# Issuing the weight-piece loads from ScalarE's queue in a hybrid decoder step

## The chip, the cores and the metric

The kernel runs on one core of one Trainium2 chip. The metric is the device time of one execution in microseconds (us), lower is better. All times below come from the profile of the kernel before, or from its timed runs.

## What is computed

One inference step of one decoder layer, in float32, for a prompt of 2048 tokens (width 1024) and for a sample group of 8 single tokens with states carried in. The layer projects each token with `w_in` (1024 x 3336), splits the result into eight RWKV-7 heads and eight Mamba-2 heads, runs both recurrences, concatenates, projects with `w_out` (1024 x 1024), adds the scaled input and normalises, then runs a squared-ReLU MLP with `w_ff1` (1024 x 4096) and `w_ff2` (4096 x 1024), adds and normalises again. Outputs are both token groups and all new states. In outline:

```python
proj = x @ w_in
o_r, wkv = rwkv7_mix(shifted(proj[:1792]), ...)
o_m, conv, ssm = mamba2_mix(proj[1792:], ...)
h = layer_norm(ALPHA * x + concat(o_r, o_m) @ w_out)
y = layer_norm(ALPHA * h + square(relu(h @ w_ff1)) @ w_ff2)
```

## The kernel before

The prompt is cut into four blocks of 512 tokens. The first stage projects the four blocks one after the other (`project`, L358 on), with the mixers of block 0 set between its matmuls. Then each block has a tail (`tail`): the `w_out` product, the first normalisation, 32 transposes into the layout that the MLP wants, the MLP in groups of four hidden tiles, the second normalisation. While the tail of one block runs, the mixers of the next block (RWKV chunks, Mamba chunks, the post-processing) are set between its matmuls by `drive`, and the sample group's work rides along in the first tail. The last tail has no mixers beside it.

Every large matmul is done in a split form for accuracy: an operand is held as a high and a low half (float32r), and three matmuls (`mm3`, L166, L167, L168) make one product. So every weight has to be split on the chip. This is done piece by piece, each time it is used, by `wpiece`: a piece of 128 partitions x 512 (256 KB) is loaded into a tile of the pool `wr` (L206); ScalarE copies it with rounding to the high half of a tile of the pool `w` (L199, in `split`); VectorE, or GpSimd for every fourth piece of the projection and every second one of the first part of a tail (`POOLA`, `POOLO`), subtracts that from the raw piece for the low half (L200). TensorE then reads both halves. The pool `wr` has 7 buffers and the pool `w` has 8, so a load can start when the subtraction seven pieces earlier in that pool is done, and a copy can start when TensorE has read the piece eight earlier.

The activations take the same way: `load_act` loads slices of x or of the mixers' output into the same pool `wr` (L322), and `split` makes the halves. The weights of a step that does not go through `wpiece` (`wdt`, L353; the small up-projections, L290) are loaded elsewhere.

All transfers are issued by SyncE (SP): weight pieces, x and mixer slices, and the mixers' scratch transfers, which move tiles through DRAM to change their layout: eight stores (L640) and eight loads (L645) per RWKV chunk, chunk loads (L621 to L626), broadcasts (L539, L542), Mamba loads (L802, L804), stores of outputs (L1229, L1165), and so on. SP works through its queue in order: an issue that waits for a buffer holds everything behind it. So do the other engines.

The order of each engine's queue is not written by hand. The tile framework orders the instructions when the program is built, from their priority (place in the program) and its own estimate of when each can start; it also sets the semaphore waits. ScalarE's queue holds the copies, the evictions of the projections (L425, L475, L476), the relu and square of the MLP (L1454, L1455), the normalisations (L1221), the transposes' evictions (L1346) and the small copies of the recurrence (L720, L732, L700).

Of the kernel before, what the change touches and what calls it, by code (L numbers as in the profile page):

```python
# [108 lines left out]
class K:  # L109
# [92 lines left out]
    def wpiece(self, src, shape, tag="w"):  # L202

        n = int(np.prod(shape))
        raw = self.sb(tag + "r", (128, 512))
        self.nc.sync.dma_start(raw[:, :n], src)  # L206
        hl = self.sb(tag, (128, 2, 512), F32R)
        self.npiece += 1
        r = {"a": POOLA, "o": POOLO, "f": POOLF}[self.pf]
        pool = r and self.npiece % r == 0  # L210
        self.split(raw[:, :n], hl[:, 0, :n], hl[:, 1, :n], self.nc.gpsimd if pool else None)
        return [hl[:, i, :n].rearrange("p (a b) -> p a b", a=shape[0]) for i in range(2)]
# [1416 lines left out]
```

## Time and profile before

| | |
|---|---|
| time, median of 3 runs | 2891.64 us (2886.47 to 2894.46) |
| the profiled execution's own time | 2881.87 us |
| its span, first to last instruction | 2880.1 us |
| mean granted TensorE clock | 0.982 of full speed |
| TensorE matmuls busy | 2786.3 us, 97% |
| VectorE busy | 1979.4 us, 69% |
| ScalarE busy | 1285.9 us, 45% |
| GpSimd busy | 364.5 us, 13% |
| 16 DMA engines, hardware queue | 45.4% |

The profiled execution is 9.8 us (0.3%) below the median of the timed runs. A busy share counts the time in which at least one instruction of that kind runs on the engine; waiting, and the issuing of a transfer, does not count. PEclk in the rows is the granted clock of TensorE: 1.00 is 2.4 GHz and 0.50 is 1.2 GHz, and a number between them is a mean over the stretch.

### The profile page before, as it was taken

To read this page: it belongs to the slowest core of one execution; us is meant where nothing else is said; L and a number is where in the kernel's file an instruction comes from. 1 tells how busy PE (TensorE), PEld (TensorE's weight loads), DVE (VectorE), ACT (ScalarE), POOL (GpSimd) and SP (SyncE) were. 2 spreads that over 40 slices of the span, in tenths; PEclk is the share of its full clock that TensorE was granted. 3 is DMA by queue.
4 is the path that set the end of the run, shared out by engine and by line. 5 is a ranking of instruction groups with operands and counts; after the bars stand their busy time and mean duration, and the time that the engine had idled before them with its cause. 6 is when DMAs were issued, how large, how long until landed. Compare 5 with 4: busy or idle time off the path is not lost.

```text
span 2880.1 us, 52319 instructions
## 1 busy us (share of the span) xinstructions
PE 2786.3 (97%) x19114; PEld 2310.9 (80%) x19114; DVE 1979.4 (69%) x4841; ACT 1285.9 (45%) x2493; POOL 364.5 (13%) x508
## 2 busy tenths in 40 slices
PE   9999999999989999998899999998999999899997
PEld 7798987777878777787788888887777778888886
DVE  7878878878777767676866666568766656754446
ACT  5554644554536333434544444336343334543332
POOL 2322212222321000002200000022000001200001
PEclk9999999999989999998999999999999999899999
DMA  6655655555744434346434344254443335433232
GB/s 207 191 169 150 185 152 165 156 176 160 211 138 133 131 110 130 110 125 215 136 93 120 115 116 121 85 196 131 120 138 114 109 103 167 158 103 95 88 103 70
DMA packets 333766, 395.54 MB, mean 137 GB/s; under 512 B 84990, under 2 KB 191060, under 8 KB 333500
## 3 DMA queue, kind: packets, MB, share of 16 engines
q1 hardware_dynamic: 333508, 392.20, 45.4%
q8 instruction: 150, 2.46, 0.4%
q14 instruction: 108, 0.88, 0.1%
HBM read 331.32 MB, written 60.81 MB: 136 GB/s over the span
## 4 chain that ended last, share of the span: by engine, by line
PE 79%; DVE 10%; DMA 4%; issue 4%; ACT 2%; SPq 1%; POOL 0%; DVEq 0%; POOLq 0%; ACTq 0%
PE psb L166 18%; PE psb L167 18%; PE psb L168 17%; PE psm L152 7%; PE psa L166 4%; PE psa L168 4%; PE psa L167 4%; PE psc L152 2%; PE psa L152 2%; PE psb L152 1%; DVE w L200 1%; PE psm L173 1%; PE psy L741 1%; DVE lr L655 1%; DVE rX L656 1%
## 5 line engine op out<-in xcount | busy, mean ns | idle before, releaser
L199 ACT ACTIVATE w<-wr 128x512 fp32r<-128x512 f32 (+1 forms) x836 | 518.8, 627 | 604.5 <-PE psb L168 237.2
L200 DVE TENSOR_TENSOR w<-wr,w 128x512 fp32r<-128x512 f32 x712 | 510.8, 722 | 230.3 <-ACT w L199 226.5
L166 PE MATMUL psb<-act,w 128*128 128x512 f32 (+2 forms) x1768 | 628.4, 356 | 6.3 <-ACT act L199 5.5
L167 PE MATMUL psb<-act,w 128*128 128x512 f32 (+2 forms) x1768 | 621.1, 352 | 0.6 <-DVE act L200 0.6
L168 PE MATMUL psb<-act,w 128*128 128x512 f32 (+2 forms) x1768 | 616.9, 349 | 0.0
L166 PEld LDWEIGHTS psb<-act,w 128*128 128x128 f32 x1768 | 335.9, 190 | 55.5 <-ACT act L199 6.0
L168 PEld LDWEIGHTS psb<-act,w 128*128 128x128 f32 x1768 | 336.3, 190 | 45.6 <-DVE w L200 0.2
L167 PEld LDWEIGHTS psb<-act,w 128*128 128x128 f32 x1768 | 337.0, 191 | 44.7 <-DVE act L200 2.6
L166 PE MATMUL psb<-w,g 128*128 128x512 f32 x788 | 317.0, 404 | 9.5 <-ACT w L199 9.5
L167 PE MATMUL psb<-w,g 128*128 128x512 f32 x788 | 314.6, 399 | 0.0
L168 PE MATMUL psb<-w,g 128*128 128x512 f32 x788 | 312.5, 397 | 0.0
L200 POOL TENSOR_TENSOR w<-wr,w 128x512 fp32r<-128x512 f32 x124 | 180.2, 1458 | 717.5 <-ACT w L199 703.6
L1504 DVE TENSOR_TENSOR g<-psb,g 128x512 f32<-128x512 f32 x173 | 118.8, 687 | 163.2 <-PE psb L168 162.6
L166 PEld LDWEIGHTS psb<-w,g 128*128 128x128 f32 x788 | 148.6, 189 | 46.1 <-ACT w L199 10.3
L168 PEld LDWEIGHTS psb<-w,g 128*128 128x128 f32 x788 | 148.4, 188 | 33.6 <-DVE g L200 0.2
L167 PEld LDWEIGHTS psb<-w,g 128*128 128x128 f32 x788 | 149.0, 189 | 32.5 <-DVE w L200 0.2
L200 DVE TENSOR_TENSOR g<-r,g 128x256 fp32r<-128x256 f32 (+1 forms) x172 | 97.1, 565 | 82.5 <-ACT g L199 81.6
L1454 ACT ACTIVATE r<-psb 128x512 f32<-128x512 f32 (+2 forms) x130 | 63.2, 487 | 190.2 <-PE psb L168 188.3
L166 PE MATMUL psa<-act,w 128*128 128x256 f32 (+2 forms) x336 | 116.4, 346 | 0.0
L167 PE MATMUL psa<-act,w 128*128 128x256 f32 (+2 forms) x336 | 114.6, 341 | 0.0
L168 PE MATMUL psa<-act,w 128*128 128x256 f32 (+2 forms) x336 | 114.1, 340 | 0.0
L655 DVE TENSOR_TENSOR lr<-rX,lr 128x4 f32<-128x4 f32 (+14 forms) x480 | 100.7, 210 | 10.8
(389 smaller groups left out, 5207.3 us busy)
## 6 DMA issues: line engine op xcount, KB each, us to landing
wr<-in_w_ff_dram SPq DMA_DIRECT2D x512, 256.0 KB
wr<-in_w_in_dram SPq DMA_DIRECT2D x208, 256.0 KB
wr<-in_w_out_dram SPq DMA_DIRECT2D x112, 256.0 KB
lr<-d_l SPq DMA_DIRECT2D x256, 64.0 KB
s_m<-g SPq DMA_DIRECT2D x48, 256.0 KB
ms<-s_m SPq DMA_DIRECT2D x16, 768.0 KB
wr<-in_xT_dram SPq DMA_DIRECT2D x32, 256.0 KB
s_ar<-g SPq DMA_DIRECT2D x16, 512.0 KB
```

The source lines that it names most:

```text
L152: return self.nc.tensor.matmul(out, l, r, start=start, stop=stop)
L166: nc.tensor.matmul(out, l[0], r[0], start=first, stop=False)
L167: nc.tensor.matmul(out, l[0], r[1], start=False, stop=False)
L168: nc.tensor.matmul(out, l[1], r[0], start=False, stop=last)
L173: self.nc.tensor.transpose(out, in_, self.cst[p0:p0 + k, o + p0:o + p0 + k])
L199: nc.scalar.activation(hi, raw, AF.Copy)
L200: (eng or nc.vector).tensor_tensor(out=lo, in0=raw, in1=hi.bitcast(F32), op=ALU.subtract)
L655: nc.vector.tensor_tensor(out=row, in0=X[:, :, s + 1:16], in1=row, op=ALU.mult)
L656: nc.vector.tensor_reduce(X[:, :, s:s + 1], lr[:, :, 17 * s:16 * s + 16], axis=AX.X, op=ALU.add)
L741: acc = lambda o, l, r, start, stop: nc.tensor.matmul(o, l, r, start=start, stop=stop, skip_group_check=True)
L1454: nc.scalar.activation(rl, ps, AF.Relu)
L1504: self.nc.vector.tensor_tensor(out=h, in0=ps, in1=h, op=ALU.add)
```

## The change

The load in `wpiece` (L206) is issued from ScalarE's queue in place of SP's. That is 832 loads of 256 KB: 208 of `w_in`, 112 of `w_out` and 512 of the two MLP matrices. All other transfers stay on SP, those into the pool `wr` by `load_act` and `wdt` among them. No buffer count and no arithmetic changes.

```diff
 raw = self.sb(tag + "r", (128, 512))
-self.nc.sync.dma_start(raw[:, :n], src)
+self.nc.scalar.dma_start(raw[:, :n], src)
 hl = self.sb(tag, (128, 2, 512), F32R)
```

## Rows read from the trace of the kernel before

**Rows 1.** The first line of the page: busy time, share of the span and number of instructions of each engine.

```profile
PE 2786.3 (97%) x19114; PEld 2310.9 (80%) x19114; DVE 1979.4 (69%) x4841; ACT 1285.9 (45%) x2493; POOL 364.5 (13%) x508
```

**Rows 2.** Busy time by stage: the stretch in us from the span's start, its length, then the busy time and number of instructions of each engine, the granted TensorE clock, the share of the DMA engines, and GB/s.

```profile
0.00:775.00 775.00, 757.38 (x5110) 624.41 (x5111) 612.61 (x1505) 393.60 (x737) 187.71 (x338) 1.00 0.60 174
775.00:885.00 110.00, 96.06 (x881) 88.23 (x879) 74.61 (x209) 46.40 (x92) 26.32 (x25) 0.89 0.46 144
885.00:1300.00 415.00, 412.20 (x2757) 327.95 (x2753) 292.79 (x747) 171.50 (x330) 13.70 (x22) 1.00 0.43 125
1300.00:1460.00 160.00, 141.08 (x1018) 122.99 (x1017) 119.96 (x279) 82.88 (x167) 34.12 (x27) 0.88 0.49 161
1460.00:1940.00 480.00, 475.64 (x3850) 405.87 (x3850) 306.57 (x813) 205.11 (x460) 32.17 (x37) 1.00 0.41 121
1940.00:2030.00 90.00, 80.12 (x633) 70.02 (x632) 77.56 (x197) 54.10 (x111) 16.46 (x13) 0.94 0.45 146
2030.00:2430.00 400.00, 397.92 (x2790) 315.81 (x2789) 256.38 (x677) 154.83 (x291) 17.05 (x24) 1.00 0.39 118
2430.00:2530.00 100.00, 90.54 (x645) 84.52 (x644) 73.06 (x140) 55.40 (x105) 25.98 (x16) 0.91 0.47 160
2530.00:2800.00 270.00, 270.00 (x1171) 218.77 (x1169) 118.68 (x178) 101.71 (x172) 0.00 (x0) 1.00 0.33 101
```

**Rows 3.** The waits of TensorE's matmuls over the whole span: who waited <- for whom, us in total, times, longest us.

```profile
PE psb L166 <- ACT w L199: 13.9, 5, 9.3
PE psb L173 <- DVE g L1308: 9.9, 4, 4.7
PE psb L166 <- ACT act L199: 5.5, 2, 5.2
PE psb L167 <- DVE w L200: 4.4, 1, 4.4
```

**Rows 4.** The view of line L206, the loads that the change moves: count, duration of one issue on SP's queue in ns (shortest/median/longest), start of the first and the last in us; and the first line of who waited for their landing (us, times).

```profile
L206 SPq DMA_DIRECT2D wr<-in_w_ff_dram x512: 327/328/1325, 839.7 to 2826.9; - x171
L206 SPq DMA_DIRECT2D wr<-in_w_in_dram x208: 327/382/1230, 0.7 to 750.5; - x104
L206 SPq DMA_DIRECT2D wr<-in_w_out_dram x112: 327/332/1325, 756.0 to 2469.8; - x112
...
  ACT w L199: 47.3, 42
```

**Rows 5.** The view of the tiles `wr`: the copies on ScalarE and the two kinds of subtraction, with duration in ns (shortest/median/longest).

```profile
L199 ACT ACTIVATE w<-wr x836: 239/632/655, 3.5 to 2843.3; 128x512 fp32r<-128x512 f32 x168
L200 DVE TENSOR_TENSOR w<-wr,w x712: 209/691/1793, 4.2 to 2844.0; 128x512 fp32r<-128x512 f32 x178
...
L200 POOL TENSOR_TENSOR w<-wr,w x124: 1262/1302/2252, 13.6 to 2489.5; 128x512 fp32r<-128x512 f32 x124
```

**Rows 6.** The waits of SP's queue ahead of these loads: us in total, times, longest us.

```profile
SPq L206 <- DVE w L200: 594.9, 319, 31.9
...
SPq L206 <- POOL w L200: 55.9, 50, 4.2
```

**Rows 7.** The three largest kinds of wait of ScalarE: us in total, times, longest us.

```profile
ACT w L199 <- PE psb L168: 237.2, 167, 8.5
ACT r L1454 <- PE psb L168: 188.3, 104, 13.3
ACT w L199 <- PE psa L168: 175.2, 52, 8.5
```

**Rows 8.** The busy time of the instructions on tiles `wr` alone, summed over the four stretches 775 to 885, 1300 to 1460, 1940 to 2030 and 2430 to 2530 us.

```profile
sum 460.00, DVE 80.68 ACT 97.32 POOL 85.89; mean DVE 20.17 ACT 24.33 POOL 21.47
```

**Rows 9.** SP's queue from 825 us in order of time: start, us, engine, line, operation, out<-in, count.

```profile
825.65 3.62 SPq L640 DMA_DIRECT2D d_l<-sc  x8
829.37 4.50 SPq L645 DMA_DIRECT2D lr<-d_l  x8
833.96 2.74 SPq L206 DMA_DIRECT2D wr<-in_w_out_dram  x6
```

**Rows 10.** From the chain of work in the same stretch: start, us, transfer.

```profile
833.45 2.26 DMA lr<-d_l
835.85 3.57 DMA wr<-in_w_out_dram
```

**Rows 11.** Busy time from 845 to 875 us, columns as in Rows 2.

```profile
845.00:875.00 30.00, 27.55 (x195) 25.30 (x195) 20.10 (x66) 15.51 (x35) 5.07 (x5) 0.77 0.58 187
```

**Rows 12.** SP's queue around 1308 us in order of time, ahead of the weight loads that follow the first tail's last wait.

```profile
1307.10 1.09 SPq L1068 DMA_DIRECT2D d_y<-lr  x2
1308.29 0.54 SPq L322 DMA_DIRECT2D wr<-s_o  x1
1308.88 0.90 SPq L206 DMA_DIRECT2D wr<-in_w_ff_dram  x2
```

**Rows 13.** The start of the span in order of time: SP's first and second weight load, and TensorE's first matmul with the wait ahead of it in brackets.

```profile
0.73 0.40 SPq L206 DMA_DIRECT2D wr<-in_w_in_dram  x1
...
3.07 0.43 SPq L206 DMA_DIRECT2D wr<-in_w_in_dram  x1
...
5.19 0.79 PE L166 MATMUL psb<-act,w 128*128 128x512 f32 x1 [5.19 <-ACT act L199]
```

**Rows 14.** SP's queue in the first stage: an instruction that the program has only in the sample group's work (L1200), which the code reaches after all four projections.

```profile
36.12 0.80 SPq L1200 DMA_DIRECT2D out_dram<-in_state_conv_dram  x1
```

## The prediction, made before the changed kernel was run

> **What bounds the kernel now.** I read the engines' shares first [rows 1]. TensorE's matmuls are busy 97% of the span; VectorE stands at 69%, ScalarE at 45%. So the bound is TensorE, and a change on another engine moves the time only where it makes TensorE wait or ends a wait. The table by stage [rows 2] says where that is. Idle is length minus matmul time. In the four long stretches between the changes of stage (885 to 1300, 1460 to 1940, 2030 to 2430, 2530 to 2800) it is 2.8, 4.4, 2.1 and 0.0 us, 9.3 us in 1565 us. In the four short stretches at the start of each tail's transposes and MLP (775 to 885, 1300 to 1460, 1940 to 2030, 2430 to 2530) it is 13.9, 18.9, 9.9 and 9.5 us: 52.2 us in 460 us, with the clock at 0.88 to 0.94. The first 775 us lose 17.6 us. The rest lies after the last weight load. The reader is to see that only the short stretches, and a little of the first stage, can answer to this change.
>
> Next, who ends TensorE's waits [rows 3]. The largest kind is a weight copy of ScalarE, 13.9 us, but 9.3 us of it is one wait; then a VectorE addition, 9.9 us; the start-up, 5.5 us nearly all in one; and one late subtraction, 4.4 us. No steady wait on ScalarE shows. Last, the loads themselves [rows 4]: copies waited for their landing 47.3 us in 42 cases out of 832 loads, and those are waits of ScalarE, not of TensorE. The loads run far enough ahead.
>
> **The change part by part.**
>
> *Removed from SP:* 832 issues. Their medians are 328 ns for 512, 382 ns for 208 and 332 ns for 112 [rows 4]: 168 + 79 + 37 = 284 us. With the longer ones among them I take 0.38 us each, 317 us. SP computes nothing, so this is worth something only where another SP transfer, or a weight load behind one, was late for TensorE. I find three places. At 825 us, sixteen scratch issues take 3.62 + 4.50 us and six weight loads stand behind them [rows 9]; the matmul that then waits 4.4 us waits for a weight's subtraction [rows 3]. At 1307 us, two sample stores and one slice load stand ahead of the weight loads until 1308.88 [rows 12], and the 9.3 us wait falls there; the slot is freed by a subtraction of VectorE, so only about 1.2 us of it is SP's. At the start, the second weight load goes out at 3.07 us behind slice loads [rows 13]; TensorE starts at 5.19 us and waits there for an activation slice, so I give 0.5 us. Sum of the three: 6.1 us at most. I take 4 us, since in the first place VectorE is busy with the recurrence too.
>
> Here the trace and a rule part. SP's sixteen issues took 8.1 us, while the load behind them landed in 2.26 us and a weight load in 3.57 us [rows 9, 10]: issuing was the longer part. The Trainium skill, page "DMA: Bandwidth & Descriptors", section "Issuing engines are not separate DMA queues", says that transfers of all issuing engines share the same DMA engines and that issuing from several saves only sequencer time, usually small beside the transfer. By the page the credit would be near nothing and the sum 9 us over the median where the rows make it 5; the rows measure this kernel, so I go by them.
>
> *Added to ScalarE:* 832 issues in its queue. No row shows an issue on ScalarE. Lower bound: nothing, if ScalarE's sequencer issues while the engine finishes an activation. Upper bound: the 317 us of SP's rows. I take SP's price, the nearest row. ScalarE then goes from 1286 to 1603 us, 56% of the span. What covers it: in the long stretches ScalarE is itself waiting for TensorE. It waited 237.2 + 175.2 us for a free `w` tile and 188.3 us for a matmul result ahead of a relu [rows 7]; an issue of 0.38 us in front of a relu that waits 1.8 us on average (188.3 / 104) costs nothing. Those stretches lost 9.3 us in 1565 us and I add nothing there. In the short stretches, work on pieces and slices takes ScalarE 97.32 us [rows 8]; at 632 ns each [rows 5] that is 154 copies, so about 154 issues, 59 us. ScalarE goes there from 238.8 us (the sum of four rows) to 298 of 460 us, 65%, still under VectorE's 345 us, 75% [rows 2]. If each issue delayed TensorE, 59 us; if none, 0. TensorE is idle 11% of these stretches (52.2 / 460), and I charge the issues at that share: 7 us. In the first stage, 208 issues at 0.38 are 79 us; TensorE is idle 2.3% there (17.6 / 775): 2 us.
>
> *A wait moved:* each of these issues waits until the subtraction seven loads earlier has freed the slot. On SP this was a wait of 594.9 us in 319 cases for VectorE and 55.9 us in 50 cases for GpSimd [rows 6], and held nothing that computes. On ScalarE it holds evictions, copies and the recurrence's small copies, for which TensorE waits. It is free if the issue stands in ScalarE's queue at a point where the subtraction is done anyway. That the order is made so shows in SP's queue, which takes what is ready and not what the program has next: a transfer of the sample group goes out at 36.12 us, in the first stage [rows 14]. A subtraction lasts 0.69 us on VectorE and 1.30 us on GpSimd [rows 5]. I charge nothing for this part and price the other case below.
>
> *Bytes* stay as they are, and so does the depth of the buffers.
>
> **Sum.** 2881.9 us of the profiled execution (span 2880.1) + 7 + 2 - 4 = 2887 us. The median of the timed runs is 9.8 us above the profiled execution; on its scale the forecast is 2891.6 + 5 = **2897 us**, 0.2% more. A measurement of this kernel can tell about 0.3%, 8.7 us, from no change, so this is no measurable change.
>
> **The rivals.**
>
> *Slower: the slot wait blocks ScalarE.* Place: the four short stretches, where half the subtractions of a tail's first part go to GpSimd, and VectorE is 75% busy. If 38% of the issues (319 / 832) meet a wait of 1.86 us (594.9 / 319), 154 of them add 59 waits, 110 us, beside 59 us of issuing: ScalarE comes to 408 of 460 us, 89%, and passes VectorE. If TensorE sees a quarter of the 169 us, 42 us: 2934 us. For it: the wait on SP is real, and ScalarE's evictions of the transposes stand in the same queue. Against it: SP reaches each wait early because it has nothing else to do, so its 1.86 us are too long for ScalarE. It decides where ScalarE's share in these stretches passes VectorE's.
>
> *Faster: SP was holding TensorE.* The 4.4 us wait at 840 us goes, with 1.2 us at 1308 and 0.5 us at the start. Behind the first, the clock is 0.77 for 30 us [rows 11]; if the wait goes and the clock stays at 2.4 GHz, 0.23 x 30 = 7 us more. 2891.6 - 13 = 2879 us. For it: sixteen issues in a row ahead of weight loads occur once per chunk. Against it: VectorE's waits remain in the same places, and a clock falls for them as well.
>
> *The run-ahead is lost.* If the order put each issue right ahead of its own copy, every copy would wait for a landing of 3.57 us [rows 10]: 832 x 3.57 = 2970 us on top of 1286, and the kernel would take over 4200 us. SP's order [rows 14] speaks against it. 2 in 100, left out of the range.
>
> **How the numbers follow.** No measurable change 0.38, slower 0.34 (of it 0.02 for the lost run-ahead), faster 0.28. A new order of all queues, by the framework's own estimate, can move single waits of 5 us either way; that is why the middle case does not get more. The range runs from two waits like that at 840 us saved (2 x 12 = 24 us under the median, 2868) to the slower rival with a little more of its 169 us seen (54 us over, 2945). Of the middle case the own range is 2883 to 2900.
>
> **What would show it.** After the change, SP's queue has no L206 and ScalarE's has 832 of them, at 0.3 to 0.4 us. ScalarE's busy time stays near 1286 us, since issuing does not count. Right: the long stretches lose under 15 us again and TensorE's waits for ScalarE stay near 20 us; the 4.4 us wait for a subtraction is gone or smaller. Wrong to the slow side: new waits of ScalarE at L206 for VectorE or GpSimd, and TensorE's waits for evictions (L1346, L1454) or small copies (L720, L732) over 20 us in total, or idle time in the long stretches. Wrong to the fast side: the short stretches lose under 40 us and their clock is above 0.95. An issue of 1 us or more on ScalarE would break the price on which all of this rests.

## The result: 0.7% slower

The changed kernel takes 2906.59 us, median of 8 runs (2898.02 to 2913.48), beside 2885.81 us for the kernel before on the same chip (8 runs). The ratio is 1.0068, 95% interval 1.0052 to 1.0085: some 20 us, more than twice the 8.7 us that the prediction took as the least to be told from no change. The profiled execution took 2901.37 us, with a span of 2899.5 us and a mean granted clock of 0.983 (0.982 before).

The first line of the page after, beside [rows 1]: the busy time of TensorE rises by 6.4 us. Its idle time, span minus busy, rises from 93.8 to 106.8 us. That makes up the 19.4 us by which the span grew. No other engine got busier; ScalarE shows nothing of its 832 issues, since issuing is not counted.

```profile
PE 2792.7 (96%) x19114; PEld 2311.2 (80%) x19114; DVE 1977.0 (68%) x4841; ACT 1277.9 (44%) x2493; POOL 358.6 (12%) x508
```

The loads after, beside [rows 4], with the same columns. The issues stand in ScalarE's queue (ACTq) with a median of 0.33 us. The first line is the one to read: 516 semaphore instructions ahead of loads, up to 2.53 us long, now in ScalarE's queue. When the queue comes to one of them it stands until the slot is free. SP's queue had 736 of them before, up to 31.8 us long, and held nothing that computes.

```profile
L206 ACTq EVENT_SEMAPHORE  x516: 17/17/2530, 15.3 to 2556.9; - x172
L206 ACTq DMA_DIRECT2D wr<-in_w_ff_dram x512: 333/334/1612, 836.2 to 2847.2; - x171
L206 ACTq DMA_DIRECT2D wr<-in_w_in_dram x208: 334/335/1491, 0.7 to 768.4; - x104
L206 ACTq DMA_DIRECT2D wr<-in_w_out_dram x112: 334/335/1672, 771.7 to 2496.1; - x112
...
  ACT w L199: 69.0, 52
```

The table by stage after, with the columns of [rows 2]. The last lines cover the same clock times, not quite the same work, since the kernel lags by up to 20 us.

```profile
0.00:775.00 775.00, 750.99 (x5059) 619.30 (x5060) 604.37 (x1495) 386.91 (x726) 177.06 (x334) 0.99 0.59 170
775.00:885.00 110.00, 98.51 (x862) 89.53 (x861) 77.03 (x213) 50.13 (x97) 31.26 (x28) 0.95 0.56 169
885.00:1300.00 415.00, 409.63 (x2790) 326.15 (x2789) 289.81 (x747) 170.69 (x334) 14.66 (x22) 1.00 0.44 124
1300.00:1460.00 160.00, 138.79 (x967) 116.94 (x966) 117.28 (x265) 76.28 (x149) 33.97 (x27) 0.90 0.50 161
1460.00:1940.00 480.00, 472.87 (x3823) 403.14 (x3822) 306.92 (x827) 204.91 (x470) 23.93 (x32) 0.99 0.39 116
1940.00:2030.00 90.00, 83.06 (x669) 74.03 (x668) 74.84 (x169) 51.33 (x104) 22.36 (x15) 0.94 0.47 156
2030.00:2430.00 400.00, 398.28 (x2791) 316.35 (x2790) 258.13 (x695) 154.21 (x294) 16.40 (x25) 1.00 0.38 113
2430.00:2530.00 100.00, 88.09 (x596) 78.89 (x595) 69.62 (x137) 48.01 (x82) 27.50 (x18) 0.93 0.54 179
2530.00:2800.00 270.00, 267.52 (x1210) 218.67 (x1209) 121.97 (x183) 108.77 (x199) 0.51 (x1) 0.99 0.32 100
```

Length minus matmul time: the four short stretches together are idle 51.5 us (52.2 before), the long ones 16.7 (9.3 before), the first stage 24.0 (17.6 before). So what was lost in idle time was lost where the prediction charged 0 and 2 us.

Stretches of equal length hide a shift, so I also compared the start of the same matmul (the n-th of lines L166 to L168, counted in both traces). After is behind by 4.7 us at 118 us, 12.7 at 690, 17.4 at 790; then only 4.1 at 890; 8 at 1348, 12.7 at 1697, 12.5 at 2384, and 19.6 from 2529 us to the end. Two things stand side by side: losses of 17 us up to 790 us and of 16 us from 890 us on, and between them **a gain of 13 us**, at the place that the faster rival had named. Of the late loss, 8 us fall in one spot: the kernel is 12.5 us behind at 2384 and 20.9 us behind at 2430 us. From 845 to 875 us, beside [rows 11], the clock is 0.89 in place of 0.77:

```profile
845.00:875.00 30.00, 24.38 (x229) 22.86 (x228) 25.82 (x90) 19.51 (x42) 10.18 (x9) 0.89 0.44 116
```

TensorE's waits after, beside [rows 3]. The one wait of 4.4 us for a subtraction (`PE psb L167 <- DVE w L200`) and the one of 9.3 us for a copy are gone; the longest for a copy is now 1.4 us. In their place stand a wait of 5.3 us for a scratch load of the sample group (at 1314 us, where the 9.3 us wait was), more for the transposes' evictions (L1346: 9.1 us in 8 waits, 4.1 us in 6 before), and many of 1 to 2 us: counted in the trace, matmul gaps between 1 and 3 us go from 17 (30 us) to 28 (46 us). Summed by engine, the waits for ScalarE are 31.1 us after and 29.9 before. No single wait carries the loss.

```profile
PE psb L173 <- DVE g L1308: 9.7, 4, 3.6
PE psb L166 <- ACT act L199: 7.5, 2, 5.9
PE psm L152 <- issue: 6.9, 8, 1.8
PE psm L173 <- DMA m<-d_y: 6.5, 2, 5.3
PE psb L166 <- ACT w L199: 6.3, 7, 1.4
...
PE psa L173 <- ACT r L1346: 3.6, 2, 2.5
PE psb L166 <- ACT r L1346: 3.0, 3, 1.5
```

**How an issue shows in ScalarE's queue.** Three short pieces of the timeline after: start, us, engine, line, operation, tile, and in brackets the idle time before it and what ended it. In the first, the load goes out 0.01 us after a copy has started, and the copy runs on for 0.63 us: the issue is covered.

```profile
24.88 0.63 ACT L199 ACTIVATE w<-wr 128x512 fp32r<-128x512 f32 x1 [0.47 <-DMA wr<-in_w_in_dram]
24.89 0.34 ACTq L206 DMA_DIRECT2D wr<-in_w_in_dram  x1
```

In the second it is not. GpSimd's subtraction ends at 791.79, the load that needed its slot goes out at 791.82, and only then can the weight copy (792.25) and the activation copy (792.79) behind it start; a matmul has waited 1.57 us for the latter. The sign is the bracket of the copy at 792.25: "POOL w L200" is no operand of it. The only link is the load ahead of it in the queue.

```profile
790.50 1.29 POOL L200 TENSOR_TENSOR w<-wr,w 128x512 fp32r<-128x512 f32 x1 [3.43 <-PE psb L168]
791.82 0.33 ACTq L206 DMA_DIRECT2D wr<-in_w_out_dram  x1
792.25 0.63 ACT L199 ACTIVATE w<-wr 128x512 fp32r<-128x512 f32 x1 [1.84 <-POOL w L200]
792.79 0.61 ACT L199 ACTIVATE act<-wr 128x512 fp32r<-128x512 f32 x1
...
793.46 0.39 PE L166 MATMUL psb<-w,act 128*128 128x256 f32 x1 [1.57 <-ACT act L199]
```

The third piece is the spot where the 8 us fall, the change into the last tail. Before, SP issued the last four loads of an MLP matrix in one go, and their copies were done by 2423.1:

```profile
2415.59 2.41 SPq L206 DMA_DIRECT2D wr<-in_w_ff_dram  x4
```

After, three of the four go out 4.4 us and more behind the first, because in ScalarE's queue they stand behind five slice copies, the relu, its square and a weight copy. The slot of the second had been free since 2428.67, when the third slice's subtraction ended. So these loads are late by their place in the queue, and the copies wait for their landing:

```profile
2428.02 0.33 ACTq L206 DMA_DIRECT2D wr<-in_w_ff_dram  x1
...
2432.47 0.89 ACTq L206 DMA_DIRECT2D wr<-in_w_ff_dram  x2
2433.40 0.45 ACTq L206 DMA_DIRECT2D wr<-in_w_ff_dram  x1
...
2435.23 0.63 ACT L199 ACTIVATE w<-wr 128x512 fp32r<-128x512 f32 x1 [1.76 <-DMA wr<-in_w_ff_dram]
2438.09 0.63 ACT L199 ACTIVATE w<-wr 128x512 fp32r<-128x512 f32 x1 [2.24 <-DMA wr<-in_w_ff_dram]
2440.52 0.63 ACT L199 ACTIVATE w<-wr 128x512 fp32r<-128x512 f32 x1 [1.80 <-DMA wr<-in_w_ff_dram]
```

Added up over the whole trace, ScalarE's queue stood at 544 loads for 442 us in total, the longest 5.0 us. Of it, 274 us ended with a weight's subtraction, most of the rest with other work of VectorE. Much of it is time in which ScalarE had nothing else ready. Waits of ScalarE's own instructions that end with a subtraction they don't read come to 60 us; the six largest lines follow. The same view of before has 3.5 us ended by a weight's subtraction.

```profile
ACT w L199 <- POOL w L200: 15.6, 8, 2.7
ACT w L199 <- DVE w L200: 13.9, 16, 2.0
ACT g L571 <- DVE w L200: 7.1, 5, 2.4
ACT r L1454 <- DVE w L200: 4.0, 2, 2.9
ACT g L425 <- POOL w L200: 3.1, 2, 1.8
ACT g L425 <- DVE w L200: 3.0, 1, 3.0
```

### The profile page after: what moved, and what is told of

Same layout as the page of the kernel before. It is cut to its first block, busy times and chain, and to the rows that moved or that the text cites. A ratio compares the mean times of both kernels' runs of the same rounds, so it can differ in the third digit from the quotient of the medians.

```text
span 2899.5 us, 51804 instructions
## 1 busy us (share of the span) xinstructions
PE 2792.7 (96%) x19114; PEld 2311.2 (80%) x19114; DVE 1977.0 (68%) x4841; ACT 1277.9 (44%) x2493; POOL 358.6 (12%) x508
## 4 chain that ended last, share of the span: by engine, by line
PE 56%; DVE 7%; DMA 5%; issue 1%; ACT 1%; SPq 0%; ACTq 0%; DVEq 0%; POOL 0%; POOLq 0%
PE psb L166 12%; PE psb L167 12%; PE psb L168 11%; PE psm L152 5%; PE psa L166 4%; PE psa L167 4%; PE psa L168 4%; DMA wr<-in_w_ff_dram 2%; PE psc L152 2%; DVE w L200 1%; PE psy L741 1%; PE psm L173 1%; DMA wr<-in_w_out_dram 1%; PE psb L152 1%; DVE m L953 1%
## 5 line engine op out<-in xcount | busy, mean ns | idle before, releaser
L200 DVE TENSOR_TENSOR w<-wr,w 128x512 fp32r<-128x512 f32 x712 | 510.6, 724 | 242.4 <-ACT w L199 237.2
L166 PE MATMUL psb<-act,w 128*128 128x512 f32 (+2 forms) x1768 | 630.4, 357 | 10.9 <-ACT act L199 5.9
L167 PE MATMUL psb<-act,w 128*128 128x512 f32 (+2 forms) x1768 | 621.9, 352 | 0.0
L168 PE MATMUL psb<-act,w 128*128 128x512 f32 (+2 forms) x1768 | 618.9, 351 | 0.0
L166 PEld LDWEIGHTS psb<-act,w 128*128 128x128 f32 x1768 | 337.5, 191 | 61.1 <-ACT act L199 5.9
L168 PEld LDWEIGHTS psb<-act,w 128*128 128x128 f32 x1768 | 337.1, 191 | 46.5 <-DVE w L200 0.9
L167 PEld LDWEIGHTS psb<-act,w 128*128 128x128 f32 x1768 | 338.1, 191 | 43.7 <-DVE act L200 1.3
L166 PE MATMUL psb<-w,g 128*128 128x512 f32 x788 | 316.7, 404 | 6.0 <-ACT w L199 4.4
L167 PE MATMUL psb<-w,g 128*128 128x512 f32 x788 | 314.4, 399 | 0.5 <-DVE w L200 0.5
L168 PE MATMUL psb<-w,g 128*128 128x512 f32 x788 | 312.5, 397 | 0.0
L200 POOL TENSOR_TENSOR w<-wr,w 128x512 fp32r<-128x512 f32 x124 | 179.4, 1451 | 619.1 <-ACT w L199 582.6
L166 PEld LDWEIGHTS psb<-w,g 128*128 128x128 f32 x788 | 148.1, 188 | 44.6 <-ACT w L199 7.2
L167 PEld LDWEIGHTS psb<-w,g 128*128 128x128 f32 x788 | 148.9, 189 | 34.4 <-DVE w L200 1.7
L168 PEld LDWEIGHTS psb<-w,g 128*128 128x128 f32 x788 | 148.4, 188 | 34.5 <-DVE g L200 0.2
L200 DVE TENSOR_TENSOR g<-r,g 128x256 fp32r<-128x256 f32 (+1 forms) x172 | 94.6, 551 | 81.7 <-ACT g L199 81.2
L1454 ACT ACTIVATE r<-psb 128x512 f32<-128x512 f32 (+2 forms) x130 | 63.3, 489 | 196.4 <-PE psb L168 165.5
L166 PE MATMUL psa<-act,w 128*128 128x256 f32 (+2 forms) x336 | 116.1, 346 | 0.0
L167 PE MATMUL psa<-act,w 128*128 128x256 f32 (+2 forms) x336 | 114.6, 341 | 0.0
L168 PE MATMUL psa<-act,w 128*128 128x256 f32 (+2 forms) x336 | 114.5, 341 | 0.0
L166 PE MATMUL psb<-g,w 128*128 128x256 f32 (+2 forms) x312 | 104.3, 334 | 1.6 <-DVE g L428 1.6
```

The lines of the kernel that those rows point to most:

```text
L166: nc.tensor.matmul(out, l[0], r[0], start=first, stop=False)
L167: nc.tensor.matmul(out, l[0], r[1], start=False, stop=False)
L168: nc.tensor.matmul(out, l[1], r[0], start=False, stop=last)
L200: (eng or nc.vector).tensor_tensor(out=lo, in0=raw, in1=hi.bitcast(F32), op=ALU.subtract)
L1454: nc.scalar.activation(rl, ps, AF.Relu)
```

## The experiments

Four theories: **A**, loads go out later at the start (the second weight load at 5.24 us, 3.07 before [rows 13]) and at the stage changes. **B**, each issue costs ScalarE its 0.33 us. **C**, the slot wait holds what is queued behind the load. **D**, the framework orders every queue anew, and the new order is worse in itself. Each time is the median of 4 to 12 runs; the ratio is to the kernel before on the same chip, which took 2881 to 2886 us.

| kernel | loads issued on | us | ratio, 95% interval |
|---|---|---|---|
| the change | ScalarE | 2906.6 | 1.0068 (1.0052 to 1.0085) |
| e1 | ScalarE, `w_in` alone | 2896.0 | 1.0038 (1.0020 to 1.0056) |
| e2 | ScalarE, all but `w_in` | 2891.1 | 1.0021 (1.0012 to 1.0031) |
| e3 | ScalarE, the first 20 on SP | 2905.3 | 1.0071 (1.0051 to 1.0090) |
| e4 | ScalarE, load raised in priority | 2930.3 | 1.0155 (1.0133 to 1.0177) |
| e5 | SP, load raised in priority | 2927.2 | 1.0136 (1.0118 to 1.0153) |
| e6 | ScalarE, behind the copy 5 pieces before | 2897.6 | 1.0043 (1.0028 to 1.0059) |
| e7 | ScalarE, in two halves | 2927.3 | 1.0140 (1.0121 to 1.0158) |
| e8 | ScalarE, 10 buffers, behind the copy 7 before | 2887.0 | 1.0004 (0.9992 to 1.0016) |
| e9 | SP, in two halves | 2894.4 | 1.0045 (1.0031 to 1.0059) |
| e10 | SP, 10 buffers | 2861.4 | 0.9926 (0.9914 to 0.9938) |
| e11 | ScalarE, 10 buffers | 2894.2 | 1.0037 (1.0022 to 1.0051) |
| e12 | as e6, in two halves | 2913.1 | 1.0105 (1.0090 to 1.0120) |

**e1 and e2: which loads.** The change for one group of loads at a time (e2 has the two engines exchanged).

```diff
-self.nc.scalar.dma_start(raw[:, :n], src)
+(self.nc.scalar if self.pf == "a" else self.nc.sync).dma_start(raw[:, :n], src)
```

> Only the 208 loads of w_in go out on ScalarE's queue; the 624 loads of the tails stay on SP's. Before is 2886 us, the full change 2907. Theory A (a load in ScalarE's queue goes out late wherever that queue stands on a wait ahead of it, above all at the start, where the median time from a load's issue to its copy fell from 17.6 to 7.0 us): the loss at the start shows here, plus 5 us, 2891, and nothing of the losses in the tails. Theory B (each issue costs ScalarE its 0.36 us): a quarter of 21 us, 2891. Theory C (waits for a free slot hold ScalarE): under 2 us, since the trace of the changed kernel shows 17 us of such waits in all. Theory D (the framework's new order of all queues moves single waits by chance): anything within 10 us. A and B are not told apart by this one, the place of the loss is.

> The complement: the 624 loads of w_out and of the MLP on ScalarE's queue, w_in on SP's. A: the start is as before (first matmul near 5.2 us, no 5 us loss in the first 120 us), the losses between 1300 and 1600 us and at 2430 to 2530 us stay, plus 14 to 15 us, 2900. B: three quarters of 21 us, plus 15, 2901, spread over the tails. D: not the sum of the parts; this and the run with w_in alone would not add up to 21 us within 5.

The 208 loads of the first stage cost 0.38%, 11 us; the 624 of the tails 0.21%, 6 us. Together that is nearly the whole 0.68%, and the prediction had it the other way round. But the 6 us are a balance. By the start of the same matmul, e2 is 2.4 us behind at 790 us, 11.0 ahead at 890 and 9.9 behind at the end: the tails gain 13 us in that one stretch and lose 21 us after it. e1 is 13.2 us behind at 790 us.

**e3: theory A at the start.**

```diff
-self.nc.scalar.dma_start(raw[:, :n], src)
+(self.nc.sync if self.npiece < 20 else self.nc.scalar).dma_start(raw[:, :n], src)
```

> The full change, but the first 20 loads (the first ten projection tiles of block 0) stay on SP. A: the start is as before, 5 us off the 2907: 2902. B: 20 issues of 832 are 0.5 us, 2906. D: unknown, but then the first 120 us need not be what recovers.

No gain shows in the time, though the two intervals leave room for 7 us, more than the 5 that A named. The trace says more: at 60 us e3 is 0.6 us behind the kernel before, where the change is 4.0; at 300 us it is 6.7 behind, where the change is 6.8. What the early loads save at the start is lost again inside the first stage.

**e4 and e5: earlier in the order,** on ScalarE and, as the control, on SP (the kernel before with the same edit).

```diff
-self.nc.scalar.dma_start(raw[:, :n], src)
+with self.tc.high_priority(RANK):
+    self.nc.scalar.dma_start(raw[:, :n], src)
```

> The full change with the load given a high priority, so that it stands earlier in ScalarE's queue: 12 rows or more ahead of its own copy in nine loads of ten, where the changed kernel has 5. The number of issues and their place on ScalarE stay. A: loads go out earlier, half of the loss or more comes back, 2896 or less, and the time from issue to copy at the start and after 2430 us is longer than the 7 us of the changed kernel. B: no change, 2907. C: ScalarE stands more often at a load whose slot is not free; waits at the load rise from 17 us to over 60 and the time to 2915 or more.

> The kernel before with the same high priority on the load that the hoisted run had, but issued by SP. Hoisting on ScalarE gave 2930 against 2884 before. Theory C (a load that waits for its slot holds what stands behind it in ScalarE's queue; added up from the traces, ScalarE's queue stood 442 us at such loads in the changed kernel, 604 us in the hoisted one): on SP the same waits hold nothing that computes, 2880 to 2892. Theory D (the new order of the queues is what costs, wherever the issue stands): 2905 to 2930.

e4 is slower still, which gives A no support. But the control loses 1.36% (39 us) without a load on ScalarE's queue, so the raised priority itself does the harm, and e4 is no test of A. Whether it does so by another order of everything (D) is not shown: SP's queue also stood longer at loads in e5, 818 us for the subtractions of weights where it was 651 before [rows 6], and the scratch transfers stand behind them. Between e4 and e5 there is 0.19%, uncertain by 0.28%: in that order the move to ScalarE costs little or nothing, though ScalarE's queue stood 604 us at loads in e4. The time at loads alone is therefore no measure of the loss.

**e6: theory C.** Each load is ordered behind the copy five pieces earlier, later in ScalarE's queue, where its slot is more often free. `cps` is the list of the copies; the lines that fill it are left out here. The edit orders the queue and adds no semaphore.

```diff
-self.nc.scalar.dma_start(raw[:, :n], src)
+with self.tc.issue_after(self.cps[-5].ins) if len(self.cps) >= 5 else ExitStack():
+    self.nc.scalar.dma_start(raw[:, :n], src)
```

> The full change, but each load is set in ScalarE's queue behind the copy of the piece five before it, by which time the subtraction seven before is mostly done. C: the time that ScalarE's queue stands at loads falls from 442 to under 250 us and the kernel takes 2898 or less. A (late loads cost; two runs spoke against it already): loads go out later, 2910 or more. B: as the full change, 2905.

As C expected: the time at loads, added up as before, falls from 442 to 99 us, and 0.25% (7 us of the 20, uncertain by 6 to 7) comes back, although the loads now go out later and more copies wait for their landing (102.7 us, 69.0 in the change). The loads' view of e6 (two of its lines are the ones to compare: semaphores ahead of loads, and who waited for them):

```profile
L209 ACTq EVENT_SEMAPHORE  x388: 17/17/1908, 15.1 to 2548.5; - x194
...
  ACT w L200: 102.7, 70
```

The traces, one execution of each, say where C holds. Up to 790 us the time at loads falls from some 150 to 50 us, and the loss by the same matmul from 17.4 to 7.6 us. From 890 us on the time at loads falls as well, from some 270 to 50 us, but e6 loses 17.9 us there where the change loses 15.7. So the slot wait explains some 10 us of the first stage and, by these traces, nothing of the tails. The spot at 2384 to 2430 us costs 8.4 us in e6, 8.8 in e2 and 8.4 in the change, and 0.1 in e1, whose tail loads are on SP: A, which e3 did not bear out at the start, holds there.

**e7, e9 and e12: theory B.** Each load as two issues of 256 columns: on ScalarE (e7), on SP as the control (e9), and on ScalarE with e6's order (e12).

```diff
-self.nc.scalar.dma_start(raw[:, :n], src)
+for s in (slice(0, n // 2), slice(n // 2, n)):
+    self.nc.scalar.dma_start(raw[:, s], src[:, s])
```

> The full change with every load issued as two halves of 256 columns, both on ScalarE: 1664 issues, the same bytes in rows of half the length. B (each issue costs ScalarE its 0.36 us; 299 us in all): as much again as the full change cost, 2927. C: the second half finds its slot free, so only little is added, 2905 to 2913.

> The kernel before, its loads still on SyncE's queue, each issued as two halves of 256 columns: the control of e7, which did the same on ScalarE's queue and took 2927 us. If a load issue costs ScalarE its time (B), the 20 us that e7 lay above the change are ScalarE's alone, and this kernel stays near the kernel before (2886, to 2892 with twice the work of SyncE). If e7's loss comes from the halves themselves (twice the descriptors and another order of the queues, D), this kernel loses about as much: 2900 to 2910.

> e6 (each load on ScalarE's queue ordered behind the copy of the piece five before, 2897.6 us) with each load issued as two halves: twice the issues of ScalarE with little slot wait. If the issue time counts (B), it lies 15 to 20 us above e6, 2913 to 2918. If it is hidden and the slot wait counts (C), it stays within 5 us of e6, 2895 to 2903. The control for the halves themselves is e9.

By itself e7 hit B's number. The control takes most of it away: on SP the same halves cost 0.45%. On ScalarE they add 0.72% to the change (e7) and 0.62% to e6 (e12). So 832 more issues cost ScalarE 0.27% and 0.17% beyond the halves, 8 and 5 us, each uncertain by some 8 us (intervals in quadrature). At their full 0.33 us they would be 278 us. B is worth 5 to 8 us of the 20, and may be nothing. A further issue is nearly always covered. That holds for a second issue right behind the first; no run measured the price of the first by itself.

**e8, e10 and e11: more buffers.** `wr` with 10 buffers in place of 7: with late loads on ScalarE (e8), on SP (e10), and on ScalarE with nothing else (e11).

```diff
-BUFS = (("wr", 7), ("w", 8), ("act", 8), ("g4", 12), ("r", 2), ("blk", 4),
+BUFS = (("wr", 10), ("w", 8), ("act", 8), ("g4", 12), ("r", 2), ("blk", 4),
```

> The full change with ten raw buffers in place of seven and each load set behind the copy of the piece seven before it: the run-ahead of the full change, and a slot that was freed about three pieces earlier. C: the queue stands at loads for under 200 us, 2885 to 2895. B: 2905. D: anything between 2880 and 2915, and the waits do not tell which.

> The kernel before with 10 raw buffers in place of 7, loads on SyncE: the control of e8. If the slot wait in ScalarE's queue is the loss (C), e8 came back to the kernel before because its loads no longer waited there, and more buffers do little for SyncE, on which only loads and stores stand: 2880 to 2888. If buffers by themselves speed the kernel up (another order, D, or earlier loads, A), this one is well under the kernel before, 2865 to 2878, and e8 still carries a cost of ScalarE's queue of about the difference.

> The change with 10 raw buffers in place of 7 and nothing else: the half of e8 that is depth alone. By C what counts is how long a load stands in ScalarE's queue: with three more buffers the slot is free earlier against the same program order unless the framework moves the load forward by as much. If the order follows the buffers' release, the waits stay and so does the loss (2900 to 2908); if the loads keep their place, waits fall to a third and the time to 2887 to 2895. By B (issue time alone) 2904 to 2908 whatever the waits. Its time together with its waits is the reading.

e8 equals the kernel before, and without its controls it would have closed the case: no slot wait, no loss. The controls say otherwise. The buffers alone, on SP, make the kernel **0.74% faster**, the best version here and ahead of both kernels. Against that, ScalarE's queue costs 1.15% with 10 buffers (2894.16 / 2861.35, same chip: 33 us), and still 0.8% with late loads (1.0004 / 0.9926). The time at loads in e11 is 459 us, as in the change: the framework moved the loads forward with the buffers (median time from a load's issue to its copy between 885 and 1300 us, added up from the traces: 21.8 us in the change, 32.7 in e11). Late order gives back 0.33% here (e11 to e8) beside 0.25% with 7 buffers (the change to e6): 10 and 7 us, each uncertain by 5 to 7.

Where 10 buffers gain on SP: the table of e10 at 775 us, beside the first short stretch of [rows 2] and of after. The clock is 0.97 and idle 10.0 us (0.89 and 13.9 before). The same matmuls are even with before at 790 us and 11 us ahead at 890.

```profile
775.00:885.00 110.00, 100.04 (x988) 91.66 (x987) 79.73 (x226) 55.85 (x116) 27.66 (x26) 0.97 0.52 163
```

The gain is mostly clock: 0.08 more over 110 us is an estimated 9 us, beside 4 us less idle time. The wait itself is nearly as long as the 4.4 us of [rows 3], although the loads were issued further ahead:

```profile
PE psa L167 <- DVE w L200: 3.4, 1, 3.4
```

In both traces the subtraction that ends it stands on VectorE among steps of the recurrence (L655, L656; it starts at 844.46 us in e10, at 843.81 before). So this wait is not shown to be SP's doing.

And what ScalarE's queue keeps: TensorE's waits in e11. The line for `m<-d_y` stands near 6 to 8 us in the change, e6, e8 and e11 and not in before or e10, but also in e9, with 4.6 us, and in e5, with 3.1, where every load is on SP. That fits D; no run isolates it. The waits for "issue", for which the profile names no cause, do go with the queue: 2.7 to 3.7 us in the four kernels with every load on SP (before, e5, e9, e10), 4.8 to 9.6 us in all others. Both belong to small steps of the mixers and the sample group, not to a weight.

```profile
PE psm L173 <- DMA m<-d_y: 7.6, 2, 6.2
...
PE psm L152 <- issue: 7.4, 6, 2.3
```

## Why the prediction was right or wrong

The forecast was +0.2%, no measurable change; the result is +0.7%, on the slower side, inside the range. The three cases were near even, and the likeliest one did not come.

- **The bound, right.** TensorE stayed at 96%, and the loss is its idle time (13.0 us) and busy time (6.4 us).
- **The price of an issue, right in size:** 0.33 us for 0.38. That it is mostly covered by a running activation was offered as the lower bound; the doubled loads give 8 and 5 us for 832 further issues, near the 9 us that the sum charged.
- **The slot wait charged at nothing: the step that failed in the sum.** "It is free if the issue stands in ScalarE's queue at a point where the subtraction is done anyway" was right as a condition, but the proof, SP's order [rows 14], says only that SP's queue is not in program order. On ScalarE the condition was missed at 544 loads. Ordering the loads later is worth 7 to 10 us, the largest term that an experiment isolates, and by the traces it is worth that in the first stage alone. The second thing that the sum left out is the run-ahead lost at a change of stage: 8 us in one spot, where loads stand in ScalarE's queue behind activations. The prediction had priced only its loss everywhere.
- **Where it falls, wrong.** The short stretches were to pay 7 us and kept their idle time (52.2 to 51.5 us). The first stage, charged 2 us, paid 11 (e1). There GpSimd makes every fourth subtraction, at 1.30 us, and evictions for the mixers stand behind the loads. The share of TensorE's idle time in a stage of before said nothing about what a new wait would do to it.
- **SP's relief, right in place, too small, and its cause in doubt.** The 4.4 us wait went, and with the higher clock the stretch gained 13 us where I credited 4 and the faster rival 12 for it. It was spent elsewhere. The rival's chance should have been part of the sum, as a gain beside a loss. But e10 gains 11 us there with every load on SP and keeps 3.4 us of the wait. What held in the sum is its reservation that VectorE is busy with the recurrence.
- **The page's rule.** The Trainium skill, page "DMA: Bandwidth & Descriptors", section "Issuing engines are not separate DMA queues", says that issuing from several engines saves only the time of the issue, usually small. The runs bear this out so far: the net result is a loss, and the one gain, 13 us, is not shown to be SP's time, since e10 has 11 of it. The reading that issuing was the longer part [rows 9, 10] set sixteen issues beside one landing; the 2.26 us are the last of the sixteen loads itself, and one issue took 8.1 / 16 = 0.5 us.
- **The slower rival** had the mechanism and the wrong size and place: 42 us in the short stretches, against 7 to 10 us in the first stage. In those stretches ScalarE was busy 226 of 460 us (issues not counted) and VectorE 339.
- **The signs named.** Long stretches idle 16.7 us, just over the 15 that were to mark the loss; new waits at L206, present; waits for evictions and small copies (L1346, L1454, L720, L732) under 20 us, so that sign failed to show it.

**What stays open.** With 7 buffers the loss is 20 us on top of a 13 us gain. So some 33 us of loss are to be explained. Late loads return 7 to 10, issues are 5 to 8 by the doubled loads, each of these with an error nearly as large as itself; the late loads at 2384 to 2430 us make 8, read from traces, and no run moved them alone. The rest, roughly a third, and about half of the 33 us with 10 buffers, is not tied to one mechanism. e5 shows that raising the loads' priority can cost more than all of it, but no kernel here held the order fixed and moved only the issues, so D is argued and not shown as the remainder.

## What to carry to other kernels

Here an issue on a computing engine cost little, since the engine mostly ran something beside it. Two other things cost: the load's wait, which holds everything queued behind it, and the load's own place behind the engine's work, which sends it out late at a change of stage. Before moving a load, look at what it waits for on its old queue, and try a few more buffers there: here they gave 0.74% where the move lost 0.68%. And run the control for each edit on the old queue: two of the experiments (e7, e8) hit a theory's number for a reason that the control (e9, e10) took away.

## What the runs showed of the hardware

- A load issue on ScalarE starts 0.01 us after an activation has started and runs 0.33 us beside it (24.88 and 24.89 us above).
- The same bytes in half-size loads cost 0.45% even from SP's queue (e9); the DMA packets rose from 333,766 to 453,585, and the median issue of a `w_ff` load on SP from 0.33 to 0.42 us.
- Delaying a load on ScalarE's queue paid 0.25%, uncertain by 0.23% (e6), though more copies then waited for its landing (102.7 us, 69.0 in the change).
